# S5 tables made in their final layout from transposed powers kept in DRAM

## The chip, the cores and the metric

The kernel runs on one core of a Trainium2 chip. The metric is the device time of one execution in microseconds; three runs of the kernel before gave 1785.19 to 1787.87 us, median 1787.56.

## The reference

The program computes two layers over 512 tokens of width 2048, batch 1. Each layer is h + RMSNorm(Mixer(RMSNorm(h))). The first mixer is an S5 state-space layer, the second forgetting attention with 16 heads. The change touches the state-space part alone, with 128 groups of 16 channels and 64 states each:

```python
xn = rmsnorm(h, g_pre)
u, z = jnp.split(xn @ w_in, 2, axis=-1)
# per group: h_t = Abar h_{t-1} + Bbar u_t,  y_t = Re(C h_t) + D u_t
mag = jnp.exp(ar * dt)
abar_re, abar_im = mag * jnp.cos(ai * dt), mag * jnp.sin(ai * dt)
x_re = coef_re * bu_re - coef_im * bu_im      # Bbar u, bu = u B^T
x_im = coef_re * bu_im + coef_im * bu_re
_, _, h_re, h_im = lax.associative_scan(combine, (a_re, a_im, x_re, x_im), axis=1)
y = einsum(h_re, c_re) - einsum(h_im, c_im) + d_skip * uf
y = gelu(y); y = y * sigmoid(y @ w_glu + b_glu); y = y * silu(z)
return h + rmsnorm(y @ w_out, g_post)
```

## The kernel before

Phase A holds the projections u and z and the state-space layer. `K` is 16: there are 16 tiles of 128 channels, and 32 projections. A projection (`proj`, L174) is 48 matmuls of 128x512 in three parts, whose fp32 weights arrive in `wraw` and are split on ACT (`whi`) and DVE (`wlo`, L151) into two rounded halves. The state-space work of tile j is spread between the projections, and time is cut into 64 chunks of CL = 8 steps:

- `ssm_tables` (L402) makes BT, which takes the 8 inputs of a chunk to the state. DVE multiplies the powers of A (`apow`, partition = state) with Bbar (`B4`, made once for four tiles by `ssm_group`, L380) into `Bt` in three operations of 128x1024 (`Bt`, `btt`, `Bt`). PE transposes its 8 blocks (`btps`, L426), ACT evicts them into BT (L427). It then makes the rotations `rot` in three operations of 128x512.
- `ssm_kernel` (L443) makes `Et` (three operations of 128x1152), the 8 short convolution kernels `kps` on PE (L466), and `ktp`, which SP writes to the DRAM tile `kd` (L473) and reads back as the 8 blocks of `M` (L477).
- `ssm_u` (L479) scales u, writes it to DRAM as `ub` and reads it back as `U`.
- `ssm_scan` (L491) multiplies U by BT into `xps` (L499), and DVE does the rotation, the scan and the rotation back into `hst`.
- `ssm_y` (L518) adds M times U (L528, the M part, 16 matmuls) and Et times `hst` (L534, the H part, 32 matmuls) into `yps`.

`order_a` (L579) writes the sequence of these steps down by hand; the framework's scheduler then places every instruction in its engine's list, and its buffers come from pools (PSUM: 3 banks for projections, 5 for all else). In each list an instruction waits for its inputs and everything behind it waits too. SP's list holds the DMA issues of kd, M, ub, U and the group inputs; the weights go through POOL's. `rows` (L295) spreads the norms by four plain matmuls with the identity (L304), once in phase A. The powers and the phasors are computed by `ssm_params` (L310) on DVE in the first 50 us.

Of the kernel before, what the change touches and what calls it, by code (L numbers as in the profile page):

```python
# [11 lines left out]
F32 = mybir.dt.float32  # L12
# [10 lines left out]
NQ = 4  # L23
# [41 lines left out]
class Kern:  # L65
# [244 lines left out]
    def ssm_params(self, i):  # L310
        nc, NG = self.nc, self.NG
        sp = self.sp
        A, E, R, CO = self.AP, self.E, self.R, self.CO
        s1 = sp.tile([P, 16, NG], F32, tag="Bt", name="scr1")
        s2 = sp.tile([P, 17, NG], F32, tag="tmp", name="scr2")
        s3 = sp.tile([P, 15, NG], F32, tag="BT", name="scr3")
        ar, ai, ld, dt, x, t, n, r, q, mag, den, nr = (s1[:, k, :] for k in range(12))
        th3, cs3, sn3 = (s2[:, k:k + 3] for k in (8, 11, 14))
        nc.scalar.dma_start(s1[:, 0:3, :], i["ssm_a"])
# [58 lines left out]
        self.ts(E[:, :, 1, 0], E[:, :, 1, 2], -1.0, ALU.mult)  # L378

    def ssm_group(self, i, q0, nq):  # L380

        nc, sp = self.nc, self.sp
        bc = [P, nq, 32]
        B4 = self.B4 = sp.tile([P, nq, 3, 16], F32, tag="B4", name="B4")
        Ca = sp.tile([P, nq, 16, 2], F32, tag="Ca", name="Ca")
        Cb = sp.tile([P, nq, 16, 2], F32, tag="Cb", name="Cb")
        self.C4 = [v.rearrange("p q c s -> p q (c s)") for v in (Ca, Cb)]
        braw = sp.tile([P, nq, 3, 16], F32, tag="braw", name="braw")
        nc.sync.dma_start(braw[:, :, 1:3], i["ssm_b"][:, q0:q0 + nq])
        nc.sync.dma_start(Ca, i["ssm_c"][:, q0:q0 + nq])  # L390
        self.act(braw[:, :, 0], braw[:, :, 2], scale=-1.0)
        co = lambda c: self.CO[:, c, q0:q0 + nq].unsqueeze(2).to_broadcast(bc)
        two = lambda v, s: v[:, :, s:s + 2].rearrange("p q s c -> p q (s c)")
        t = sp.tile(bc, F32, tag="tmp", name="gt")
        self.tt(two(B4, 1), two(braw, 1), co(0), ALU.mult)
        self.tt(t, two(braw, 0), co(1), ALU.mult)
        self.tt(two(B4, 1), two(B4, 1), t, ALU.add)
        self.act(B4[:, :, 0], B4[:, :, 2], scale=-1.0)
        self.act(Cb, Ca[:, :, :, ::-1], scale=-1.0)
        self.act(Ca[:, :, :, 1], Ca[:, :, :, 1], scale=-1.0)  # L400

    def ssm_tables(self, i, j):  # L402

        nc, sp = self.nc, self.sp
        if j % 4 == 0:
            self.ssm_group(i, NQ * j, min(4 * NQ, self.NG - NQ * j))
        ql = NQ * (j % 4)
# [3 lines left out]
        Bt = sp.tile([P, NQ, 2, 16, CL], F32, tag="Bt", name="Bt")
        bv = Bt.rearrange("p q s c t -> p q (s c) t")
        bc = [P, NQ, 32, CL]
        pw = lambda c: self.AP[:, c, qs, 0:CL].unsqueeze(2).to_broadcast(bc)
        vv = lambda s: self.B4[:, ql:ql + NQ, s:s + 2].rearrange("p q s c -> p q (s c)").unsqueeze(3).to_broadcast(bc)
        t = sp.tile(bc, F32, tag="tmp", name="btt")
        self.tt(bv, pw(0), vv(1), ALU.mult)
        self.tt(t, pw(1), vv(0), ALU.mult)
        self.tt(bv, bv, t, ALU.add)

        BT = T["BT"] = sp.tile([P, NQ, 2, P], F32, tag="BT", name="BT")
        for q0 in range(0, NQ, 2):
            bps = self.bank(name="btps").rearrange("p (q c g) -> p q c g", q=2, c=2)
            for q in range(2):
                for c in range(2):
                    nc.tensor.transpose(bps[:, q, c, :], Bt[:, q0 + q, c].rearrange("p c t -> p (c t)"), self.ident)  # L426
            self.act(BT[:, q0:q0 + 2], bps)  # L427

        rot = T["rot"] = sp.tile([P, NQ, 3, NC], F32, tag="rot", name="rot")
        rv = rot[:, :, 1:3].rearrange("p q s (a b) -> p q (s a) b", b=8)  # L430
        bc = [P, NQ, 16, 8]
        e8 = lambda s: self.E[:, qs, 1, s:s + 2].rearrange("p q s a -> p q (s a)").unsqueeze(3).to_broadcast(bc)
        e1 = lambda s: self.E[:, qs, 0, 1 + s].unsqueeze(2).to_broadcast(bc)
        t = sp.tile(bc, F32, tag="tmp", name="rt")
        self.tt(rv, e8(1), e1(0), ALU.mult)
        self.tt(t, e8(0), e1(1), ALU.mult)
        self.tt(rv, rv, t, ALU.add)
        self.act(rot[:, :, 0], rot[:, :, 2], scale=-1.0)
        dec = T["dec"] = self.dec[j % 2]
        self.act(dec[:, :, :, 1:], self.R[:, qs].unsqueeze(2).unsqueeze(3).to_broadcast([P, NQ, 2, NC - 1]))  # L440
        return T

    def ssm_kernel(self, j, T):  # L443

        nc, sp = self.nc, self.sp
# [12 lines left out]
        bb = self.bb[j % 2]  # L458
        for h in range(2):
            ph = slice(64 * h, 64 * h + 64)  # L460
            self.act(bb[ph, :, :, h, :], self.B4[ph, ql:ql + NQ, 1:3])
# [29 lines left out]
    def ssm_scan(self, j, U, T):  # L491
# [3 lines left out]
        for q in range(NQ):  # L495
            for c in range(2):
                for g in range(2):
                    pg = slice(64 * g, 64 * g + 64)
                    nc.tensor.matmul(X[pg, q, c], lhsT=T["BT"][:, q, c, pg], rhs=U[:, 2 * q + g, :],  # L499
                                     start=True, stop=True)  # L500
        rot = T["rot"]
        bc = [P, NQ, 2, NC]
# [76 lines left out]
    def order_a(self):  # L579
# [5 lines left out]
        seq += [("u", j) for j in range(min(2, K))]  # L585
        z = n0
        seq += [("z", j) for j in range(max(1, n0 - 1), n0)]
        seq += [("tab", 0), ("ker", 0)]
        for s in range(K):
            seq.append(("scan", s))  # L590
            if s + 2 < K:
# [4 lines left out]
            if s + 1 == K:  # L596
                seq.append(("y", s))
                continue
            seq.append(("tab", s + 1))
            tail = [("y", s), ("ker", s + 1)]  # L600
            while z < K - n1 and (z - n0) < (K - n0 - n1) * (s + 1) / K:
                seq.append(("z", z))
# [5 lines left out]
    def phase_a(self, i):  # L608
        nc, K, D, tc = self.nc, self.K, self.D, self.tc
        self.NG = NQ * K  # L610
        with ExitStack() as ctx:
            sp = self.sp = ctx.enter_context(tc.tile_pool(name="ssm", bufs=1))
            self.AP = sp.tile([P, 2, self.NG, CL + 1], F32, name="apow")
            self.E = sp.tile([P, self.NG, 2, 3, 8], F32, name="phasors")
# [4 lines left out]
            xin = [("ga", 1), ("gt", 1), ("X", 1), ("Z", 1), ("rt2", 1), ("gy", 2), ("gy", 2),  # L619
                   ("u", 2), ("u", 2), ("U", 3), ("U", 3), ("U", 3), ("rot", 1), ("braw", 1),  # L620
                   ("zt", 2), ("zt", 2)]
            assert K <= len(xin)


            zero = sp.tile([P, S], F32, tag="BT", name="zero")
            nc.vector.memset(zero, 0.0)
            warm = self.bank(name="warm")
            for _ in range(5):
# [63 lines left out]
            for n, (c, j) in enumerate(seq):  # L692
# [466 lines left out]
```

## Time and profile before

| | us |
|---|---|
| median of three runs | 1787.56 (1785.19 to 1787.87) |
| the profiled run, its own time | 1786.9 |
| its span | 1785.1 |
| PE busy | 1762.5 (99%) |
| DVE busy | 1078.4 (60%) |
| ACT busy | 590.1 (33%) |
| POOL busy | 430.0 (24%) |

Phase A takes the first 430 us or so. PE is the engine for matrix products, DVE the vector engine, ACT the scalar engine; SP and POOL here issue DMAs. A row of a timeline gives start and length; a PE row's length runs past the start of the next one, so what an instruction takes is read from start to start. "x8" counts records: a plain fp32 matmul leaves two, a transpose one.

### The profile page before, as it was taken

To read this page: it belongs to the slowest core of one execution; us is meant where nothing else is said; L and a number is where in the kernel's file an instruction comes from. 1 tells how busy PE (TensorE), PEld (TensorE's weight loads), DVE (VectorE), ACT (ScalarE), POOL (GpSimd) and SP (SyncE) were. 2 spreads that over 40 slices of the span, in tenths; PEclk is the share of its full clock that TensorE was granted. 3 is DMA by queue.
4 is the path that set the end of the run, shared out by engine and by line. 5 is a ranking of instruction groups with operands and counts; after the bars stand their busy time and mean duration, and the time that the engine had idled before them with its cause. 6 is when DMAs were issued, how large, how long until landed. Compare 5 with 4: busy or idle time off the path is not lost.

```text
span 1785.1 us, 26466 instructions
## 1 busy us (share of the span) xinstructions
PE 1762.5 (99%) x10710; PEld 1493.7 (84%) x10710; DVE 1078.4 (60%) x1582; ACT 590.1 (33%) x993; POOL 430.0 (24%) x382
## 2 busy tenths in 40 slices
PE   9999999999999999999999999999999999999997
PEld 6888888888888888899888888888888888988887
DVE  9789898984655532365663666465655665552235
ACT  7233233323444422234332333233333332332231
POOL 1123333333100000013333343333343343300000
PEclk9999999999999999999999999999999999999999
DMA  9545555557444643342322323332223233235332
GB/s 329 151 140 158 156 161 151 146 148 242 142 144 147 209 137 96 110 148 94 94 88 89 95 89 95 95 97 92 88 89 100 89 89 96 88 129 165 102 106 95
DMA packets 126427, 226.66 MB, mean 127 GB/s; under 512 B 38496, under 2 KB 65392, under 8 KB 126048
## 3 DMA queue, kind: packets, MB, share of 16 engines
q1 hardware_dynamic: 107824, 169.59, 30.4%
q0 software_dynamic: 18192, 55.01, 10.3%
q8 instruction: 84, 1.38, 0.3%
q14 instruction: 39, 0.32, 0.1%
q10 hardware_dynamic: 288, 0.36, 0.1%
HBM read 201.88 MB, written 22.97 MB: 126 GB/s over the span
## 4 chain that ended last, share of the span: by engine, by line
PE 92%; DVE 5%; DMA 2%; issue 1%; ACT 0%; SPq 0%; POOL 0%; DVEq 0%; ACTq 0%; POOLq 0%
PE proj L170 18%; PE proj L172 18%; PE proj L171 18%; PE tok L232 6%; PE tok L231 6%; PE tok L230 6%; PE v L204 3%; PE v L205 3%; PE v L206 3%; PE yps L534 1%; PE t L943 1%; PE yps L528 1%; PE xps L499 1%; DVE wlo L151 1%; PE btps L426 1%; DVE al L75 1%
## 5 line engine op out<-in xcount | busy, mean ns | idle before, releaser
L151 DVE TENSOR_TENSOR wlo<-wraw,whi 128x1024 fp32r<-128x1024 f32 x284 | 421.1, 1484 | 461.4 <-ACT whi L84 460.2
L84 ACT ACTIVATE whi<-wraw 128x1024 fp32r<-128x1024 f32 (+2 forms) x292 | 306.0, 1049 | 873.4 <-PE proj L172 535.1
L147 POOL TENSOR_TENSOR wraw<-wraw,vecs 128x1024 f32<-128x1024 f32 (+1 forms) x128 | 263.8, 2061 | 624.5 <-DMA wraw<-kv_k 257.0
L171 PE MATMUL proj<-BH,wlo 128*128 128x512 f32 (+1 forms) x816 | 308.8, 378 | 4.3 <-DVE wlo L151 4.3
L170 PE MATMUL proj<-BH,whi 128*128 128x512 f32 (+1 forms) x816 | 310.7, 381 | 0.0
L172 PE MATMUL proj<-BL,whi 128*128 128x512 f32 (+1 forms) x816 | 308.9, 379 | 0.0
L170 PE MATMUL proj<-ah,whi 128*128 128x512 f32 x768 | 302.2, 394 | 1.3 <-ACT zt L84 1.3
L172 PE MATMUL proj<-al,whi 128*128 128x512 f32 x768 | 299.0, 390 | 0.9 <-issue 0.9
L171 PE MATMUL proj<-ah,wlo 128*128 128x512 f32 x768 | 299.2, 390 | 0.6 <-DVE wlo L151 0.6
L171 PEld LDWEIGHTS proj<-BH,wlo 128*128 128x128 f32 x816 | 154.6, 189 | 33.1 <-DVE wlo L151 5.4
L172 PEld LDWEIGHTS proj<-BL,whi 128*128 128x128 f32 x816 | 154.4, 189 | 28.8 <-DVE BL L72 0.2
L170 PEld LDWEIGHTS proj<-BH,whi 128*128 128x128 f32 x816 | 154.5, 189 | 27.5
L170 PEld LDWEIGHTS proj<-ah,whi 128*128 128x128 f32 x768 | 144.1, 188 | 33.3 <-ACT zt L84 1.7
L171 PEld LDWEIGHTS proj<-ah,wlo 128*128 128x128 f32 x768 | 144.2, 188 | 30.9 <-DVE wlo L151 1.4
L172 PEld LDWEIGHTS proj<-al,whi 128*128 128x128 f32 x768 | 144.2, 188 | 30.4
L205 PE MATMUL v<-wlo,BH 128*128 128x512 f32 (+2 forms) x320 | 111.3, 348 | 0.0
L204 PE MATMUL v<-whi,BH 128*128 128x512 f32 (+2 forms) x320 | 111.3, 348 | 0.0
L206 PE MATMUL v<-whi,BL 128*128 128x512 f32 (+2 forms) x320 | 111.3, 348 | 0.0
L230 PE MATMUL tok<-whi,BH 128*128 128x512 f32 (+1 forms) x320 | 111.1, 347 | 0.0
L230 PE MATMUL tok<-whi,ah 128*128 128x512 f32 (+1 forms) x320 | 111.0, 347 | 0.0
L232 PE MATMUL tok<-whi,al 128*128 128x512 f32 (+1 forms) x320 | 110.9, 347 | 0.0
L231 PE MATMUL tok<-wlo,ah 128*128 128x512 f32 (+1 forms) x320 | 110.9, 347 | 0.0
(213 smaller groups left out, 2395.4 us busy)
## 6 DMA issues: line engine op xcount, KB each, us to landing
wraw<-w_fox SPq DMA_DIRECT2D x64, 512.0 KB, 3.6
wraw<-w_in POOLq DMA_DIRECT2D x58, 512.0 KB, 4.3
wraw<-w_glu POOLq DMA_DIRECT2D x32, 512.0 KB, 4.5
wraw<-w_out SPq DMA_DIRECT2D x32, 512.0 KB, 3.7
wraw<-kv_k SPq DMA_DIRECT2D x32, 512.0 KB, 3.7
wraw<-w_fo SPq DMA_DIRECT2D x32, 512.0 KB, 3.6
wraw<-kv_v SPq DMA_DIRECT2D x28, 512.0 KB, 3.7
M<-kd SPq DMA_DIRECT2D x128, 64.0 KB, 2.3
```

Source lines behind the costliest of these rows:

```text
L84: self.nc.scalar.activation(out, in_, f, **kw)
L147: (eng or nc.vector).tensor_tensor(raw, raw, scale.unsqueeze(2).to_broadcast(shp), op=ALU.mult)
L151: (eng if eng and scale is None else nc.vector).tensor_tensor(lo, raw, hi, op=ALU.subtract)
L170: mm(ps, lhsT=hi, rhs=xh, start=(k == 0), stop=False)
L171: mm(ps, lhsT=lo, rhs=xh, start=False, stop=False)
L172: mm(ps, lhsT=hi, rhs=xl, start=False, stop=(k == self.K - 1))
L204: nc.tensor.matmul(o, lhsT=xh[k][:, bs], rhs=hi, start=(k == 0), stop=False)
L205: nc.tensor.matmul(o, lhsT=xh[k][:, bs], rhs=lo, start=False, stop=False)
L206: nc.tensor.matmul(o, lhsT=xl[k][:, bs], rhs=hi, start=False, stop=(k == K - 1))
L230: nc.tensor.matmul(ps, lhsT=xh[k][:, bs], rhs=hi, start=(k == 0), stop=False)
L231: nc.tensor.matmul(ps, lhsT=xh[k][:, bs], rhs=lo, start=False, stop=False)
L232: nc.tensor.matmul(ps, lhsT=xl[k][:, bs], rhs=hi, start=False, stop=(k == K - 1))
```

## The change

Powers and Bbar are turned once, instead of their product in every tile. After `ssm_params`, the new `ssm_powers` multiplies each of the 8 powers (real and imaginary) by the identity, 16 matmuls (`aps`), evicts them into `asb` on ACT and writes three tables, at_d (real, minus imaginary, imaginary), to DRAM. `ssm_group_b` makes Bbar for four tiles (`B2`), transposes it in 4 blocks (`bps`) and writes bt_d. `ssm_fetch` reads, for one tile, three blocks of at_d (`AT`) and two of bt_d (`BTab`) of 128x512 each, with rows repeated over partitions. `ssm_tables` multiplies these two straight into BT in its final layout with three operations of 128x1024, issues the fetch of the next tile, and makes `rot`. BT and rot have two buffers each, and `order_a` runs the tables two tiles ahead of the scan, one more than before. Phasors, a few buffer tags and the place of the C tables' loads change with it.

```diff
-        B4 = self.B4 = sp.tile([P, nq, 3, 16], F32, tag="B4", name="B4")
+    def ssm_powers(self):
+        nc, NG = self.nc, self.NG
+        ph, n = P // NG, CL * NG // P
+        o = self.sp.tile([P, 3, n, P], F32, tag="AT", name="asb")
+        for c in range(2):
+            ps = self.bank(name="aps").rearrange("p (n f) -> p n f", f=P)[:, :n]
+            for t in range(CL):
+                r = slice(NG * (t % ph), NG * (t % ph) + NG)
+                nc.tensor.matmul(ps[r, t // ph], lhsT=self.AP[:, c, :, t], rhs=self.ident, start=True, stop=True)
+            self.act(o[:, 2 * c], ps)
+            if c:
+                self.act(o[:, 1], ps, scale=-1.0)
+        for c in range(3):
+            nc.sync.dma_start(self.at_d[c].rearrange("(n r) q f -> (r q) n f", r=ph), o[:, c])
+
+    def ssm_group_b(self, i, n):
...
+        nc.sync.dma_start(braw, i["ssm_b"][:, q0:q0 + nq])
...
+        self.tt(t, braw[:, :, ::-1], co(self.CO[:, 2:0:-1]), ALU.mult)
+        self.tt(braw, braw, co(self.CO[:, 0:1].to_broadcast([P, 2, self.NG])), ALU.mult)
+        self.tt(B2.rearrange("p j s q -> p j q s"), jq(braw), jq(t), ALU.add)
+        ps = self.bank(name="bps").rearrange("p (j f) -> p j f", f=P)[:, :nt]
+        for j in range(nt):
+            nc.tensor.transpose(ps[:, j], B2[:, j].rearrange("p s q -> p (s q)"), self.ident)
+        o = sp.tile([P, nt, P], F32, tag="zt", name="bsb", bufs=2)
+        self.act(o, ps)
+        nc.sync.dma_start(self.bt_d[n].rearrange("j r f -> r j f"), o)
+
+    def ssm_fetch(self, j):
+        AT = sp.tile([P, 3, n], F32, tag="AT", name="AT")
+        BT = sp.tile([P, 2, n], F32, tag="BTab", name="BTab")
+        for c in range(3):
+            s = self.at_d[c]
+            nc.sync.dma_start(AT[:, c], bass.AP(s.tensor, s.offset + j * n, [[0, 16], [self.NG * P, CL], [1, n]]))
+        s = self.bt_d[j // 4][j % 4]
+        for c in range(2):
+            nc.sync.dma_start(BT[:, c], bass.AP(s.tensor, s.offset + c * 16 * n, [[n, 16], [0, CL], [1, n]]))
+        self.tabs = AT, BT
 def ssm_tables(self, i, j):
-        self.tt(bv, pw(0), vv(1), ALU.mult)
-        self.tt(t, pw(1), vv(0), ALU.mult)
-        self.tt(bv, bv, t, ALU.add)
-        BT = T["BT"] = sp.tile([P, NQ, 2, P], F32, tag="BT", name="BT")
-        for q0 in range(0, NQ, 2):
-            bps = self.bank(name="btps").rearrange("p (q c g) -> p q c g", q=2, c=2)
-            for q in range(2):
-                for c in range(2):
-                    nc.tensor.transpose(bps[:, q, c, :], Bt[:, q0 + q, c].rearrange("p c t -> p (c t)"), self.ident)
-            self.act(BT[:, q0:q0 + 2], bps)
+        AT, Bb = self.tabs
+        BT = T["BT"] = sp.tile([P, 2, n], F32, tag="BT", name="BT", bufs=2)
+        t = sp.tile([P, 2, n], F32, tag="tmp", name="btt")
+        self.tt(BT, AT[:, 0:1].to_broadcast([P, 2, n]), Bb, ALU.mult)
+        self.tt(t, AT[:, 1:3], Bb[:, ::-1], ALU.mult)
+        self.tt(BT, BT, t, ALU.add)
+        if j + 1 < K:
+            self.ssm_fetch(j + 1)
-        rot = T["rot"] = sp.tile([P, NQ, 3, NC], F32, tag="rot", name="rot")
+        rot = T["rot"] = sp.tile([P, NQ, 3, NC], F32, tag="rot", name="rot", bufs=2)
+        if j + 2 < K and (j + 2) % 4 == 0:
+            self.ssm_group_b(i, (j + 2) // 4)
 def order_a(self):
-        seq += [("tab", 0), ("ker", 0)]
+        seq += [("tab", 0), ("ker", 0)] + [("tab", 1)] * (K > 1)
-            seq.append(("tab", s + 1))
+            seq += [("tab", s + 2)] * (s + 2 < K)
```

What stands on the engines changes in more places than the diff shows. On PE, before, behind xps of tile 1 come 48 projection rows, a btps block, and then yps of tile 1 (the numbers in yps and ah name buffers; the last rows before yps):

```order
L170 MATMUL proj<-ah_269,whi 128x512
L171 MATMUL proj<-ah_269,wlo 128x512
L172 MATMUL proj<-al_270,whi 128x512
L426 MATMUL btps<-ident,Bt 128x128 x8
L528 MATMUL yps_1378<-U,M 64x64 x2
L528 MATMUL yps_1379<-U,M 64x64 x2
```

In the changed kernel, the same place, from xps of tile 1:

```order
L542 MATMUL xps<-U,BT 64x64 x16
L171 MATMUL proj<-ah_261,wlo 128x512
L172 MATMUL proj<-al_262,whi 128x512
L170 MATMUL proj<-ah_270,whi 128x512
L171 MATMUL proj<-ah_270,wlo 128x512
L571 MATMUL yps_1440<-U,M 64x64 x2
L172 MATMUL proj<-al_271,whi 128x512
L170 MATMUL proj<-ah_276,whi 128x512
L571 MATMUL yps_1441<-U,M 64x64 x2
L171 MATMUL proj<-ah_276,wlo 128x512
L172 MATMUL proj<-al_277,whi 128x512
```

The M part of yps moved from 48 projection rows behind xps to 4 rows behind it, and its pairs stand one by one between projection rows. In tile 3 it stands 5 rows behind, in tile 5 9, in tile 7 30; in tiles 9 and 11 to 15 it stands 46 or 48 rows behind, as before.

On SP, before, from the first kd write (tile 0) to the one of tile 1:

```order
L473 DMA kd<-ktp_131 128x240
L477 DMA M<-kd 128x1x128 x8
L486 DMA ub<-u 128x512
L488 DMA U<-ub 128x8x64
L473 DMA kd<-ktp_132 128x240
```

In the changed kernel, the same stretch:

```order
L516 DMA kd<-ktp_138 128x240
L443 DMA AT<-at_d_117 128x1x512
L443 DMA AT<-at_d_118 128x1x512
L520 DMA M<-kd 128x1x128 x8
L443 DMA AT<-at_d_119 128x1x512
L446 DMA BTab<-bt_d_120 128x1x512 x2
L443 DMA AT<-at_d_117 128x1x512
L443 DMA AT<-at_d_118 128x1x512
L443 DMA AT<-at_d_119 128x1x512
L446 DMA BTab<-bt_d_120 128x1x512 x2
```

The fetches of two tiles now stand between the kd write of tile 0 and that of tile 1, and the last three issues of the first of them behind the 8 issues of M.

## Rows read from the trace of the kernel before

**Rows 1.** The page's 40 slices: busy tenths of each engine

```profile
PE   9999999999999999999999999999999999999997
DVE  9789898984655532365663666465655665552235
```

**Rows 2.** One stretch: us; busy us (instructions) of PE, PEld, DVE, ACT, POOL; clock; DMA

```profile
100.00:200.00 100.00, 100.00 (x966) 83.20 (x964) 88.58 (x99) 33.70 (x60) 28.61 (x49) 1.00 0.54 153
```

**Rows 3.** Timeline of PE, tile 0: start, length, engine, line, operation

```profile
88.59 0.39 PE L171 MATMUL proj<-ah,wlo 128*128 128x512 f32 x1
...
89.05 1.03 PE L426 MATMUL btps<-ident,Bt 128*128 128x128 f32 x8
90.01 0.67 PE L466 MATMUL kps<-Et,bb 128*32 128x128 f32 x16
90.61 0.50 PE L170 MATMUL proj<-ah,whi 128*128 128x512 f32 x1
90.94 0.40 PE L171 MATMUL proj<-ah,wlo 128*128 128x512 f32 x1
...
91.51 1.15 PE L499 MATMUL xps<-U,BT 128*64 128x64 f32 x32
92.59 0.50 PE L170 MATMUL proj<-ah,whi 128*128 128x512 f32 x1
```

**Rows 4.** Timeline of PE, the norms' rows

```profile
66.34 1.06 PE L304 MATMUL rows<-ident,rs_b 128*128 128x128 f32 x8
67.16 0.47 PE L170 MATMUL proj<-ah,whi 128*128 128x512 f32 x1
```

**Rows 5.** Waits of PE, whole run: us in total, times, longest

```profile
PE proj L170 <- ACT zt L84: 1.3, 1, 1.3
PE yps L528 <- DMA M<-kd: 0.9, 1, 0.9
```

**Rows 6.** Timelines of PE and of SP's queue, and the page's DMA issues

```profile
199.76 0.39 PE L172 MATMUL proj<-al,whi 128*128 128x512 f32 x1
200.08 0.67 PE L466 MATMUL kps<-Et,bb 128*32 128x128 f32 x16
200.68 1.15 PE L528 MATMUL yps<-U,M 128*64 128x64 f32 x32
...
202.88 0.51 PE L499 MATMUL xps<-U,BT 128*64 128x64 f32 x10
...
179.12 0.32 SPq L473 DMA_DIRECT2D kd<-ktp  x1
...
201.91 0.32 SPq L473 DMA_DIRECT2D kd<-ktp  x1
205.61 5.01 SPq L477 DMA_DIRECT2D M<-kd  x8
...
221.76 0.39 SPq L473 DMA_DIRECT2D kd<-ktp  x1
...
M<-kd SPq DMA_DIRECT2D x128, 64.0 KB, 2.3
...
U<-ub SPq DMA_DIRECT2D x16, 256.0 KB, 4.4
```

**Rows 7.** Groups of DVE from 91 to 412 us: busy us, mean ns, idle before

```profile
L72 DVE TENSOR_TENSOR Bt<-apow,B 128x1024 f32<-128x1024 f32 x15 | 18.3, 1220 | 4.5 <-PE btps L426 4.2
...
L75 DVE SCALAR_TENSOR_TENSOR ktp<-eye,vecs,kps 128x16 f32<-128x16 f32 x16 | 3.6, 228 | 22.0 <-PE kps L466 22.0
```

**Rows 8.** Timeline of PE around its longest wait; 15 steps between the last two

```profile
856.91 0.28 PE L172 MATMUL proj<-BL,whi 128*128 128x256 f32 x1
857.03 0.28 PE L170 MATMUL proj<-BH,whi 128*128 128x256 f32 x1
860.90 0.58 PE L171 MATMUL proj<-BH,wlo 128*128 128x256 f32 x1 [3.60 <-DVE wlo L151]
...
864.27 0.29 PE L171 MATMUL proj<-BH,wlo 128*128 128x256 f32 x1
```

More of the change, by code (lines that the diff above doesn't have):

```diff
@@ L313, in ssm_params @@
         A, E, R, CO = self.AP, self.E, self.R, self.CO
-        s1 = sp.tile([P, 16, NG], F32, tag="Bt", name="scr1")
+        s1 = sp.tile([P, 16, NG], F32, tag="BTab", name="scr1")
         s2 = sp.tile([P, 17, NG], F32, tag="tmp", name="scr2")
-        s3 = sp.tile([P, 15, NG], F32, tag="BT", name="scr3")
+        s3 = sp.tile([P, 15, NG], F32, tag="BT", name="scr3", bufs=2)
         ar, ai, ld, dt, x, t, n, r, q, mag, den, nr = (s1[:, k, :] for k in range(12))
@@ L345, in ssm_params @@
         self.tt(CO[:, 1, :], t, den, ALU.mult)
+        self.ts(CO[:, 2, :], CO[:, 1, :], -1.0, ALU.mult)
         w1, w2 = (s2[:, x:x + 4, :].rearrange("p a g -> p (a g)").rearrange("p (g a) -> p g a", a=4) for x in (0, 4))
@@ L362, in ssm_params @@
         self.tt(R, t, t, ALU.mult)
-        c, si = E[:, :, :, 1], E[:, :, :, 2]
+        c, si = E[:, :, 0:4:3], E[:, :, 1:5:3]
         nc.vector.memset(c[:, :, :, 0], 1.0)
@@ L377, in ssm_params @@
         self.cmul(*e(slice(5, 8)), *e(slice(1, 4)), *b4, w3, w4)
-        self.ts(E[:, :, 1, 0], E[:, :, 1, 2], -1.0, ALU.mult)
-    def ssm_group(self, i, q0, nq):
-        nc, sp = self.nc, self.sp
-        bc = [P, nq, 32]
-        B4 = self.B4 = sp.tile([P, nq, 3, 16], F32, tag="B4", name="B4")
+        self.ts(E[:, :, 2], E[:, :, 4], -1.0, ALU.mult)
+        self.ssm_powers()
+    def ssm_powers(self):
[12 more added lines that the diff above has]
+            nc.sync.dma_start(self.at_d[c].rearrange("(n r) q f -> (r q) n f", r=ph), o[:, c])
@@ new lines, in ssm_group_b @@
+    def ssm_group_b(self, i, n):
+        nc, sp = self.nc, self.sp
+        nt = min(4, self.K - 4 * n)
+        nq = NQ * nt
+        q0 = 4 * NQ * n
+        braw = sp.tile([P, nq, 2, 16], F32, tag="braw", name="braw")
+        nc.sync.dma_start(braw, i["ssm_b"][:, q0:q0 + nq])
+        bc = [P, nq, 2, 16]
+        co = lambda v: v[:, :, q0:q0 + nq].rearrange("p s q -> p q s").unsqueeze(3).to_broadcast(bc)
+        t = sp.tile(bc, F32, tag="tmp", name="gt")
+        B2 = self.B2[n] = sp.tile([P, nt, 32, NQ], F32, tag="B2", name="B2", bufs=2)
+        jq = lambda v: v.rearrange("p (j q) s c -> p j q (s c)", q=NQ)
+        self.tt(t, braw[:, :, ::-1], co(self.CO[:, 2:0:-1]), ALU.mult)
[7 more added lines that the diff above has]
+        nc.sync.dma_start(self.bt_d[n].rearrange("j r f -> r j f"), o)
@@ L385, in ssm_group, with ssm_group_c @@
+    def ssm_group_c(self, i, n):
+        nc, sp = self.nc, self.sp
+        nq = NQ * min(4, self.K - 4 * n)
+        q0 = 4 * NQ * n
         Ca = sp.tile([P, nq, 16, 2], F32, tag="Ca", name="Ca")
@@ L387, in ssm_group @@
         self.C4 = [v.rearrange("p q c s -> p q (c s)") for v in (Ca, Cb)]
-        braw = sp.tile([P, nq, 3, 16], F32, tag="braw", name="braw")
-        nc.sync.dma_start(braw[:, :, 1:3], i["ssm_b"][:, q0:q0 + nq])
         nc.sync.dma_start(Ca, i["ssm_c"][:, q0:q0 + nq])
[L391 to L398, printed above, removed]
         self.act(Cb, Ca[:, :, :, ::-1], scale=-1.0)
         self.act(Ca[:, :, :, 1], Ca[:, :, :, 1], scale=-1.0)
-    def ssm_tables(self, i, j):
[L404 to L407, printed above, removed]
+    def ssm_fetch(self, j):
+        nc, sp = self.nc, self.sp
+        n = NQ * P
+        AT = sp.tile([P, 3, n], F32, tag="AT", name="AT")
[7 more added lines that the diff above has]
+        self.tabs = AT, BT
@@ L408, in ssm_tables @@
+    def ssm_tables(self, i, j):
+        nc, sp, K = self.nc, self.sp, self.K
+        if j == 0:
+            self.ssm_group_b(i, 0)
+            self.ssm_fetch(0)
+            self.ssm_group_c(i, 0)
         qs = slice(NQ * j, NQ * j + NQ)
         T = {}
[L411 to L415, printed above, removed]
@@ L429, in ssm_tables @@
-        rot = T["rot"] = sp.tile([P, NQ, 3, NC], F32, tag="rot", name="rot")
+        n = NQ * P
+        AT, Bb = self.tabs
[7 more added lines that the diff above has]
+        rot = T["rot"] = sp.tile([P, NQ, 3, NC], F32, tag="rot", name="rot", bufs=2)
@@ L430, in ssm_tables @@
         rv = rot[:, :, 1:3].rearrange("p q s (a b) -> p q (s a) b", b=8)
         bc = [P, NQ, 16, 8]
-        e8 = lambda s: self.E[:, qs, 1, s:s + 2].rearrange("p q s a -> p q (s a)").unsqueeze(3).to_broadcast(bc)
-        e1 = lambda s: self.E[:, qs, 0, 1 + s].unsqueeze(2).to_broadcast(bc)
+        e8 = lambda s: self.E[:, qs, 2 + s:4 + s].rearrange("p q s a -> p q (s a)").unsqueeze(3).to_broadcast(bc)
+        e1 = lambda s: self.E[:, qs, s].unsqueeze(2).to_broadcast(bc)
         t = sp.tile(bc, F32, tag="tmp", name="rt")
@@ L458, in ssm_kernel @@
         bb = self.bb[j % 2]
+        B2 = self.B2[j // 4][:, j % 4].rearrange("p (s c) q -> p q s c", s=2)
         for h in range(2):
             ph = slice(64 * h, 64 * h + 64)
-            self.act(bb[ph, :, :, h, :], self.B4[ph, ql:ql + NQ, 1:3])
+            self.act(bb[ph, :, :, h, :], B2[ph])
         kps = self.bank(name="kps")[:, :P]
@@ L498, in ssm_scan @@
                     pg = slice(64 * g, 64 * g + 64)
-                    nc.tensor.matmul(X[pg, q, c], lhsT=T["BT"][:, q, c, pg], rhs=U[:, 2 * q + g, :],
+                    nc.tensor.matmul(X[pg, q, c], lhsT=T["BT"][:, c, q * P + 64 * g:q * P + 64 * g + 64], rhs=U[:, 2 * q + g, :],
                                      start=True, stop=True)
@@ L613, in phase_a @@
             self.AP = sp.tile([P, 2, self.NG, CL + 1], F32, name="apow")
-            self.E = sp.tile([P, self.NG, 2, 3, 8], F32, name="phasors")
+            self.E = sp.tile([P, self.NG, 5, 8], F32, name="phasors")
+            self.at_d = [self.dp.tile([CL, self.NG, P], F32, name=f"at_d{c}") for c in range(3)]
+            self.bt_d = [self.dp.tile([min(4, K - 4 * n), P, P], F32, name=f"bt_d{n}") for n in range((K + 3) // 4)]
+            self.B2 = {}
             self.R = sp.tile([P, self.NG], F32, name="rdec")
@@ L618, in phase_a @@
             ws = [((c, j), i["w_in"][j + (K if c == "z" else 0)], None) for c, j in seq if c in "uz"]
-            xin = [("ga", 1), ("gt", 1), ("X", 1), ("Z", 1), ("rt2", 1), ("gy", 2), ("gy", 2),
-                   ("u", 2), ("u", 2), ("U", 3), ("U", 3), ("U", 3), ("rot", 1), ("braw", 1),
+            xin = [("X", 1), ("Z", 1), ("rt2", 1), ("gy", 2), ("gy", 2), ("u", 2), ("u", 2),
+                   ("U", 3), ("U", 3), ("U", 3), ("rot", 2), ("rot", 2), ("braw", 1), ("Ca", 1),
                    ("zt", 2), ("zt", 2)]
             assert K <= len(xin)
-            zero = sp.tile([P, S], F32, tag="BT", name="zero")
+            zero = sp.tile([P, S], F32, tag="BT", name="zero", bufs=2)
             nc.vector.memset(zero, 0.0)
@@ L707, in phase_a @@
                     if j == 0:
-                        self.rows(rstd, self.rstd, sp, "gt", True)
+                        self.rows(rstd, self.rstd, sp, "rt2", True)
                     U[j] = self.ssm_u(j, ps)
@@ L713, in phase_a @@
                     self.ssm_kernel(j, T[j])
+                    if j + 1 < K and (j + 1) % 4 == 0:
+                        self.ssm_group_c(i, (j + 1) // 4)
                 elif c == "scan":
```

1 line of the change is left out of this document (removed).

## Prediction

> **What bounds the kernel now.** I read first the page's slices: PE is at 9 tenths from the second slice to the last, DVE at 8 or 9 only in the first quarter [rows 1]. So the program ends when PE has worked through its list, and an instruction that leaves PE's list gives its time back unless PE then waits. Next, a table of stretches: from 100 to 200 us, where the SSM tiles run between projections, PE is busy in all 100 us and DVE in 88.6, at full granted clock and a DMA share of 0.54 [rows 2]. PE binds there, with DVE 11% behind it; every microsecond of PE's list in this stretch reaches the end. PE's waits come third: in the whole run one of 1.3 us on zt, which stands at 43 us, and one of 0.9 us on M [rows 5]. There is thus little waiting to win back, and a new wait costs its full length. The sum is made against the profiled run, 1786.9 us, 0.7 below the median of 1787.56; I make no correction for that. I call 0.2%, 3.6 us, the least difference that a measurement of this kernel can tell from none.
>
> **Work removed from PE.** 16 blocks btps of 8 transposes go. In the timeline one takes from 89.05 to 90.01, 0.96 us [rows 3]. Without it the next SSM row pays the step from a projection row that btps pays now, 0.31 (199.76 to kps at 200.08) instead of the 0.23 between projection rows (two steps from 88.59 to 89.05), 0.08 [rows 3, 6]. That leaves 0.88 each: **-14.1 us**. The 32 ACT evictions behind them go too; ACT is not what PE waits for, so they are worth nothing. The zt wait goes because aps rows and a different weight order now fill that place: **-1.3**.
>
> **Work added to PE.** ssm_powers multiplies the powers by the identity in 16 plain matmuls. The nearest rows are the four of the rows block: 66.34 to 67.16, 0.82 us, 0.205 each [rows 4], so 3.3. They stand alone at 11 places more than one, between projections; a return from a foreign block costs its first projection row 0.33 instead of 0.23 (90.61 to 90.94) [rows 3], so some 0.12 for each place, 1.4. Together **+4.7** (3.3 to 5.6). Four blocks bps of 4 transposes, half a btps block, 0.47 each: **+1.9**. The powers on DVE must be ready for aps about half a microsecond before they are now: **+0.5** (0 to 2).
>
> The trace shows that plain multiplications by the identity come out as two records each (8 for 4 matmuls, [rows 4]) and transposes as one (8 for 8, [rows 3]). The Trainium skill, "Perfetto Trace Analysis", section Transposes, asks for transposes in place of ordinary matmuls; the trace agrees. With transposes at 0.96 / 8 = 0.12 the 16 would cost 1.9 instead of 3.3; the sum keeps 3.3, since the change uses the plain form.
>
> **Work split on PE.** The order shows more than the removal: the M part of yps for tiles 1, 3 and 5 stands in 8 pairs with one or two projection rows between each, where before its 16 matmuls were one block. Rows price such a split: three projection rows between kps and xps take 90.61 to 91.51, 0.90 us, against 3 x 0.23 = 0.69 [rows 3], so 0.21 for a pair of switches. With 7 extra pairs in each of three tiles and two or three in tile 7, some 24 x 0.19: **+4.5** (2.5 to 5).
>
> **A wait that M brings.** This carries the forecast. M(j) is read back from kd, which is written from ktp, which comes from kps(j). Before, 48 projection rows stood between xps(j) and yps(j). Now kps(1), yps(0) and xps(1) stand together and only 4 projection rows follow before the first pair of yps(1); 5 in tile 3, 9 in tile 5, 30 in tile 7. PE reaches that pair after kps 0.60, yps(0) 2.20 (200.68 to 202.88), xps 1.08 and 4 rows, 1.0: 4.9 us from the start of kps [rows 3, 6]. The data: from kps at 200.08 to the issue of kd at 201.91 is 1.8, from there to the first M issue at 205.61 is 3.7, and M lands 2.3 after its issue [rows 6]. That is 7.8 us, so PE waits 2.9 in tile 1. In tile 3 it reaches the pair at 5.1 and waits 2.7, in tile 5 at 6.0 and 1.8. The 8 M issues take 5.0 us, the last starting 4.4 after the first, so it lands at 12.2; in tile 7 PE wants it at about 11.7 and waits 0.5 to 1. Sum **+8.2**. Below: kd's issue could come 1 us sooner where nothing stands ahead of ktp on DVE and ACT (kps takes only 0.60 of the 1.8), which leaves 4. Above: the extra traffic lengthens landings. The change fetches five transfers of 256 KB per tile, 1.31 MB in about 20 us, 65 GB/s on the 153 shown [rows 2]; U, of the same size, lands in 4.4 us [rows 6]. One microsecond more in each of two hops over four tiles makes 14 to 16.
>
> By the Trainium skill, "DMA: Bandwidth & Descriptors", section Anatomy of one DMA, a transfer costs about 2 us plus its bytes over 436 GB/s; an estimate from it puts kd at 2.3 and U at 2.6, where rows have 3.7 up to the next issue for kd and 4.4 for U. By the page the M waits would be about 1.4 us shorter in each of the first three tiles and gone in tile 7, some 5 in all; the rows decide.
>
> **Waits on the fetch.** SP issues in order. The last three issues of the fetch for tile 2 stand behind the 8 M issues of tile 0 (and so in later tiles). M(0) ends its issues about 1.8 + 3.7 + 5.0 = 10.5 us after kps(0); three issues of 0.5 or so and 4.4 to land make 16.5 [rows 6]. Behind it on DVE stand three table operations, three rotations and three for B2 (the first like Bt, 1.22 each [rows 7], the others half as wide, 0.6 each), 7.3 us, and between them the wlo operations, which are as wide as Bt: 24 to 26 with one or two of those. PE reaches bps of the second group 93 rows and xps later, at about 23. I take **+3** (0 to 5), and for kps of tiles 0, 2 and 4, whose Et stands behind the same DVE queue, **+2** (0 to 4). That DVE queue also holds ktp, and behind ktp the kd write, M and yps: a late fetch is passed on.
>
> **DVE close behind.** A pair of tiles takes 42.6 us (179.12 to 221.76) with 144 projection rows [rows 6]. In the new order the pairs from tile 2 to 9 hold about 121. PE's need falls to 121 x 0.23 + 2 x 4.2 = 36.2; DVE's is 0.886 x 42.6 = 37.8 less one wlo, 36.6. In these pairs PE could not run at its own pace even if M were there. The waits and splits above bring PE to some 39, so I add nothing, but it keeps the saving from being whole: DVE spends 22.0 us waiting for kps already [rows 7].
>
> **Sum.** -14.1 - 1.3 + 4.7 + 1.9 + 0.5 + 4.5 + 8.2 + 3 + 2 = +9.4, so 1796.
>
> **The rivals.**
> (a) *The data are there in time.* If M and the fetches land before PE asks, what remains is -14.1 - 1.3 + 4.7 + 1.9 + 0.5 + 4.5 = -3.8: 1783, faster. For it: M waits were 0.9 in the whole run before [rows 5], and DMA has room (share 0.54). Against: the 48 rows that hid M are gone in three tiles. It decides where M's first issue follows kd's within 0.8 us in tile 1, 1.0 in tile 3 and 1.9 in tile 5, instead of 3.7. Chance 0.16.
> (b) *The waits are half as long* (4 + 1 + 1) and the splits cost 2.5: -3.8 - 2 + 6, about no change, 1787. Chance 0.19.
> (c) *Waits drop the clock.* After a wait of 3.60 us, rows of 256 columns take 3.37 us for 15 steps, 0.225 each, where 0.12 stood between them before it [rows 8]; that is the lower level of the granted clock, 1.2 GHz, and costs 1.6. After 1.3 us at 43 us nothing like it is seen. Waits of 2.9 and 2.7 stand between. If four waits reach that length, with longer landings and M waits near 14, +9.4 + 5.8 + 6 less what overlaps, 1: 1807. Chance 0.20. The Trainium skill, "TensorE: Matmul & The Clock Gate", section Why this matters for your kernels, says that idle gaps between bursts bring the low clock back; the trace agrees.
> (d) *The change does not do what it says*, the btps time staying in another form, is excluded by the order: no btps rows stand there.
> The forecast itself, 1790 to 1801, has 0.45.
>
> **How the numbers follow.** Predicted is the forecast's 1796. Range: the low end reaches into (a), 1782, the high end to most of (c), 1806; a tenth is left out on either side. The forecast's own range is 1790 to 1801. Faster is (a), 0.16; same is (b), 0.19; slower the forecast and (c), 0.65.
>
> **What would show it.** In the new profile: no btps; aps and bps near 5 and 2 us busy; PE waits on M in yps of tiles 1, 3, 5 of 2 to 3 us each, a wait at the second bps, and DVE waits for AT or BTab. Granted clock below 1.00 in 100 to 300 us would be (c). If M waits are under 0.5 us each, the forecast's main step is wrong; if PE waits on DVE more than on M, the co-bound is what I mis-sized.

## The result, and the profile after

The change makes the kernel slower: median 1844.46 us of four runs (1840.94 to 1847.55) against 1787.71 before, a ratio of 1.0319 with a 95% interval of 1.0307 to 1.0332. The sign was forecast, the size was not: the predicted loss was 8 us and the range ended at 1806; the measured loss is 57.

The profiled run of the changed kernel took 1847.55 us, the longest of the four. Its page, with the rows that answer to [rows 1] and the granted clock under them:

```profile
PE   9998988899999999999999999999999999999997
...
DVE  8567778888365542238655566645663666552235
...
PEclk9998889999999999999999999999999999999999
```

Four of PE's slices from the fourth to the eighth have become 8s, and the granted clock stands at 8 in the fourth to sixth. That is phase A. All of the loss lies there: between the profiled runs the last yps starts its last row at 483.5 us instead of 421.6, and the first v matmul of phase D at 879.5 instead of 818.0, 61.5 later; the whole span is 60.7 longer.

The waits of PE from 75 to 500 us (total, times, longest), where before there were 0.9 on M [rows 5] and 0.9 on issue:

```profile
PE yps L571 <- DMA M<-kd: 14.5, 9, 4.3
PE kps L509 <- DVE Et L72: 8.0, 6, 3.5
PE bps L417 <- DVE B L72: 5.6, 3, 4.6
PE proj L170 <- ACT gy L84: 1.4, 1, 1.4
```

And what DVE waited for in that stretch, the table transfers, which is new:

```profile
DVE btt L72 <- DMA BTab<-bt_d: 25.5, 8, 5.0
...
DVE BT L72 <- DMA BTab<-bt_d: 8.1, 3, 3.9
```

Three stretches of 25 us with the columns of [rows 2] (us, busy us by engine, granted clock, DMA share, GB/s) show the rest:

```profile
150.00:175.00 25.00, 23.44 (x255) 16.04 (x250) 13.77 (x17) 6.44 (x11) 6.26 (x11) 0.73 0.55 151
200.00:225.00 25.00, 21.65 (x148) 14.28 (x145) 15.09 (x20) 4.63 (x9) 6.61 (x12) 0.73 0.52 144
250.00:275.00 25.00, 20.75 (x154) 13.27 (x149) 13.46 (x17) 3.09 (x7) 6.84 (x13) 0.66 0.57 156
```

PE is idle for 1.6 to 4.2 us in each, and the mean granted clock is 0.73 or less. At its lower level, 1.2 GHz, the record is 0.5, so 0.73 over 25 us is 13.5 us at that level. Summed over the 25 us stretches from 75 to 500 us, PE is idle for 31.7 us (1.8 before) and TensorE stands at 1.2 GHz for 65 us (0 before). A microsecond at half speed loses half a microsecond, so idle and clock together cost 30 + 32 = 62 us, or some 60, since 4 us of the idle lie inside stretches at 1.2 GHz and are counted twice. That is the whole loss between the profiled runs, 60.7. The work on PE is thus about as long as before. That what btps saved went into aps, bps and the split follows from the sum; no run times the split at full clock.

What this looks like on PE behind xps of tile 1, the place shown in the orders ahead of the prediction:

```profile
153.24 0.40 PE L170 MATMUL proj<-ah,whi 128*128 128x512 f32 x1
153.48 0.40 PE L171 MATMUL proj<-ah,wlo 128*128 128x512 f32 x1
155.43 0.34 PE L571 MATMUL yps<-U,M 128*64 128x64 f32 x4 [1.56 <-DMA M<-kd]
155.69 0.50 PE L172 MATMUL proj<-al,whi 128*128 128x512 f32 x1
156.03 0.40 PE L170 MATMUL proj<-ah,whi 128*128 128x512 f32 x1
156.36 0.43 PE L571 MATMUL yps<-U,M 128*64 128x64 f32 x4
156.72 0.80 PE L171 MATMUL proj<-ah,wlo 128*128 128x512 f32 x1
157.31 0.63 PE L172 MATMUL proj<-al,whi 128*128 128x512 f32 x1
157.87 0.48 PE L571 MATMUL yps<-U,M 128*64 128x64 f32 x4
158.29 0.80 PE L170 MATMUL proj<-ah,whi 128*128 128x512 f32 x1
159.01 0.48 PE L571 MATMUL yps<-U,M 128*64 128x64 f32 x4
```

The wait on M is there, 1.56 us where 2.9 was predicted (from the issue of kd at 150.73 to the first M issue at 152.52 it took 1.8 us here, not 3.7). What follows was not predicted: from 156.4 on a group of one projection row and one pair takes 1.14 us (157.87 to 159.01) and one of two rows and a pair 1.5, where the first group of two rows and a pair, still at full speed, took 0.93 (155.43 to 156.36). PE is not waiting here; it runs at half speed, and goes on so until about 170 us, some 5 us beyond the end of the M part.

### The profile page after: what moved, and what is told of

It is laid out like the page before. It is cut to its first block, busy times and chain, and to the rows that moved or that the text cites. A ratio compares the mean times of both kernels' runs of the same rounds, so it can differ in the third digit from the quotient of the medians.

```text
span 1845.8 us, 26390 instructions
## 1 busy us (share of the span) xinstructions
PE 1795.8 (97%) x10630; PEld 1500.8 (81%) x10630; DVE 1082.0 (59%) x1583; ACT 580.2 (31%) x960; POOL 420.7 (23%) x382
## 3 DMA queue, kind: packets, MB, share of 16 engines
q1 hardware_dynamic: 115360, 192.41, 33.6%
## 4 chain that ended last, share of the span: by engine, by line
PE 83%; DVE 6%; DMA 5%; SPq 2%; issue 2%; ACT 1%; DVEq 0%; ACTq 0%
PE proj L171 16%; PE proj L170 16%; PE proj L172 16%; PE tok L230 6%; PE tok L231 6%; PE tok L232 6%; PE v L205 3%; PE v L204 3%; PE v L206 3%; DMA BTab<-bt_d 3%; DVE wlo L151 1%; SPq L520 1%; DMA M<-kd 1%; PE t L992 1%; DMA kd<-ktp 1%
## 5 line engine op out<-in xcount | busy, mean ns | idle before, releaser
L147 POOL TENSOR_TENSOR wraw<-wraw,vecs 128x1024 f32<-128x1024 f32 (+1 forms) x128 | 259.7, 2029 | 635.0 <-DMA wraw<-kv_k 274.6
L170 PE MATMUL proj<-ah,whi 128*128 128x512 f32 x768 | 309.4, 403 | 1.8 <-ACT gy L84 1.4
L171 PE MATMUL proj<-ah,wlo 128*128 128x512 f32 x768 | 309.2, 403 | 0.7 <-DVE wlo L151 0.7
L172 PE MATMUL proj<-al,whi 128*128 128x512 f32 x768 | 307.5, 401 | 0.0
L171 PEld LDWEIGHTS proj<-ah,wlo 128*128 128x128 f32 x768 | 148.4, 193 | 33.9 <-DVE wlo L151 1.9
L172 PEld LDWEIGHTS proj<-al,whi 128*128 128x128 f32 x768 | 148.0, 193 | 31.1
```

The lines of the kernel that those rows point to most:

```text
L147: (eng or nc.vector).tensor_tensor(raw, raw, scale.unsqueeze(2).to_broadcast(shp), op=ALU.mult)
L170: mm(ps, lhsT=hi, rhs=xh, start=(k == 0), stop=False)
L171: mm(ps, lhsT=lo, rhs=xh, start=False, stop=False)
L172: mm(ps, lhsT=hi, rhs=xl, start=False, stop=(k == self.K - 1))
```

## The experiments

Idle and time at 1.2 GHz are sums over the stretches from 75 to 500 us of the profiled run, as above. Times are medians, against 1785 to 1788 for the kernel before, timed beside them; e1, e2, e6, e8, e9 and e10 have two runs each, e4 three, e3 and e7 four, e5 eight.

| kernel | us | profiled run | PE idle | at 1.2 GHz |
|---|---|---|---|---|
| before | 1787 | 1787 | 1.8 | 0 |
| the change | 1844 | 1848 | 31.7 | 65.0 |
| M part in one block (e1) | 1838 | 1838 | 43.4 | 45.0 |
| no fetch (e2) | 1806 | 1803 | 16.2 | 13.5 |
| tables one tile ahead (e3) | 1826 | 1831 | 35.5 | 38.5 |
| before without btps (e4) | 1778 | 1777 | 6.0 | 0 |
| e3 without fetch (e5) | 1793 | 1788 | 10.5 | 7.0 |
| fetch on ACT's queue (e6) | 1852 | 1855 | 42.7 | 61.5 |
| e3 with two buffers, fetch two ahead (e7) | 1803 | 1801 | 12.7 | 10.5 |
| e7 on ACT's queue (e8) | 1823 | 1820 | 26.9 | 31.0 |
| filler ahead of the M part (e9) | 1829 | 1828 | 29.4 | 20.5 |
| e5 with unread traffic (e10) | 1804 | 1806 | 21.6 | 21.0 |

### e1: the M part in one block

```diff
-        for q in range(NQ):
-            for h in range(2):
+        for q in reversed(range(NQ)):
+            for h in (1, 0):
...
-                                     start=(q == 0), stop=False)
+                                     start=(q == NQ - 1), stop=False)
```

> The changed kernel with the M part of yps walked from its last block to its first, so that its first matmul needs the last of the eight M transfers and its 16 matmuls stand in one block again (20, 20, 25 and 30 projection rows behind xps in tiles 1, 3, 5 and 7). Fetches and tables are untouched. Theory A (late data): PE idles because the fetch of AT and BTab comes late to DVE and M late to PE; the idle of about 32 us between 100 and 475 us stays, and so does most of the low clock: 1830 to 1845. Theory B (the split): the pairs of yps between projection rows are what keeps TensorE's clock at its lower level for 13 us at a time; without them the granted clock is near 1.00 but for a few us behind each wait, and 20 to 30 us come back: 1812 to 1825.

1838.13 us: theory A's range. Time at 1.2 GHz fell by 20 us, which is worth 10, but PE's waits on M rose by 11:

```profile
PE yps L571 <- DMA M<-kd: 25.5, 6, 6.5
```

The three stretches from above, with the M part whole:

```profile
150.00:175.00 25.00, 18.54 (x260) 15.33 (x257) 15.25 (x18) 6.42 (x11) 7.80 (x14) 0.86 0.59 152
200.00:225.00 25.00, 18.18 (x189) 14.39 (x188) 17.20 (x20) 5.37 (x9) 10.07 (x18) 0.80 0.62 169
250.00:275.00 25.00, 21.54 (x213) 17.33 (x212) 21.83 (x26) 6.32 (x11) 8.30 (x15) 0.93 0.72 199
```

In the first of them PE waits 6.46 us for M in one piece and is at 1.2 GHz for 7 us (0.86); the split M part behind a wait of 1.56 us was at 1.2 GHz for 13.5. So the split hides M's lateness and pays for it in clock; taking it away gives the lateness back as idle. It is not the root.

### e2 and e5: no fetch, with tables two tiles or one tile ahead

```diff
-        if j + 1 < K:
-            self.ssm_fetch(j + 1)
```

> The changed kernel with the fetch of AT and BTab for tile 0 alone; tiles 1 to 15 use tile 0's tables again, so 75 transfers of 256 KB are left out and with them part of what is computed. The order still splits the M part in tiles 1 and 3 and two pairs of tile 5. Theory A (late data): DVE waits for no table, bps and kps are in time, PE's idle falls from 32 to under 12 us: 1795 to 1805. Theory B (the split): the two split tiles still run at the lower clock, 6 to 8 us each, and M waits stay: 1805 to 1820. Rival C (the fetch's traffic alone lengthens all landings, M's too): also M waits vanish, 1785.

1806.12 us (1802.66 and 1809.58), at the edge between A and B: 38 us of the 57 go with the fetch. The order stayed split in tiles 1 and 3, M waits were 8.6 us, and 13.5 us at 1.2 GHz remain.

> Tables one tile ahead as before the change, and the fetch of AT and BTab left out but for tile 0 (its tables are used for all tiles, so what is computed differs): PE's order is close to that of the kernel before and DVE waits for no transfer. It gives what the new layout alone is worth. Theory A (the fetch is what costs): at or a little below the kernel before: measured -9 for btps, +4.7 and +1.9 for aps and bps, 1782 to 1790. If the change has another cost that is neither the fetch nor the order: above 1795.

1792.92 us (eight runs, 1787.8 to 1795.6; ratio 1.0042, 1.0031 to 1.0052), above A's range by 3. With a fetch for tile 0 alone and nearly the old order, the new layout does not beat the kernel before. The trace is of the fastest run, 1787.8; in it the last yps row still comes 5.7 us later than before (427.3 instead of 421.6), and the part behind phase A, which the change does not touch, was shorter in that execution. What PE waits for is little:

```profile
PE yps L569 <- DMA M<-kd: 3.7, 4, 1.9
PE kps L507 <- DVE Et L72: 3.1, 3, 2.1
PE bps L417 <- DVE B L72: 1.5, 1, 1.5
```

### e3: tables one tile ahead

```diff
-        seq += [("tab", 0), ("ker", 0)] + [("tab", 1)] * (K > 1)
+        seq += [("tab", 0), ("ker", 0)]
...
-            seq += [("tab", s + 2)] * (s + 2 < K)
+            seq.append(("tab", s + 1))
```

> The changed kernel with the tables one tile ahead, as before the change, instead of two: layout, powers through DRAM and the fetch stay. PE's order is then nearly that of the kernel before: yps 46 to 48 projection rows behind xps, no split. Theory A: the fetch still stands behind M in SP's list and takes 6.8 us to land, DVE still waits about 30 us for it, bps, kps or xps come late: 1800 to 1815. Theory B: without the split the clock stays at 1.00 and M is in time; what remains is -14 for btps, +7 for aps and bps, and a few us of waits: 1780 to 1788.

1825.73 us, ratio 1.0211 (1.0187 to 1.0234): slower than either theory's range, but on A's side. PE's order was near that of the kernel before, no M part was split, and still PE idled 35.5 us, since the table operations on DVE stood waiting (17.3 us on BTab, 14.6 more that the trace files under issue) and Et behind them:

```profile
PE kps L509 <- DVE Et L72: 11.5, 4, 5.9
PE yps L571 <- DMA M<-kd: 9.1, 6, 4.4
```

With and without the fetch the times are 1826 and 1793 one tile ahead, at 1844 and 1806 two tiles ahead. The fetch costs 33 or 38 us, the tile further ahead 19 or 13.

### e4: what btps was worth

```diff
-        for q0 in range(0, NQ, 2):
-            bps = self.bank(name="btps").rearrange("p (q c g) -> p q c g", q=2, c=2)
...
-            self.act(BT[:, q0:q0 + 2], bps)
+        T["BT"] = Bt.rearrange("p q s c t -> p q s (c t)")
```

> The kernel before with its 128 transposes btps and the 32 evictions behind them left out (xps reads the table Bt untransposed, so its numbers are others). It measures the gain alone that the change is after. By the prediction's first term -14.1 us: 1773. Rival: DVE, busy 89% of that stretch, becomes the bound and less than half comes back: above 1780.

1778.37 us, ratio 0.9954 (0.9935 to 0.9973): -9 us, between the two expectations and two thirds of the -14.1 in the sum. PE's idle rose from 1.8 to 6.0 us, for the most part in front of kps, and that is nearly all of the missing third:

```profile
PE kps L460 <- ACT gy L84: 3.5, 7, 0.5
PE yps L522 <- DMA M<-kd: 2.3, 1, 2.3
```

The btps block had covered these waits: yps, kps and the eviction of gy come closer together once it is gone.

### e6 and e8: the fetch on ACT's queue

```diff
-            nc.sync.dma_start(AT[:, c], bass.AP(...
+            nc.scalar.dma_start(AT[:, c], bass.AP(...
```

The same is done for BTab.

> The changed kernel with the fetch's DMAs issued from ACT's queue instead of SP's, so that they no longer stand behind the eight M issues; buffers and tables two tiles ahead stay. If the place in SP's list is what makes the fetch late: DVE's waits for BTab fall from 33.6 us to under 10 and the time to 1805 to 1820. If it is the landing time (6.8 us) and the single buffer, which lets the fetch start only when DVE has read the tables before: waits stay, 1835 to 1850.

1852.18 us, no better than the change itself (8 us slower). DVE's waits for BTab fell from 33.6 to 11.6 us, as the first branch expected, and the time did not: ACT now stood in its place, its whi held behind the fetch issues (35.2 us filed under M<-kd), and wlo and PE behind whi. The place in SP's list counted, but not for the end.

> The same as the run with two buffers, the fetch issued from ACT's queue. If SP's list still delays M or the fetch there, this is 5 us or more faster than that run; if only the buffer counts, within 3 us of it. ACT loses 64 issues of about 0.6 us, which PE does not wait for.

1822.88 us, 20 slower than the same kernel with the fetch on SP. Neither branch named this: ACT is not spare in this phase, since every projection's weights pass through it. Its whi operations stood waiting behind the fetch issues (33.9 us, filed under M and AT), and DVE's waits for whi rose from 47.9 us in e7 to 67.1.

### e7: two buffers, the fetch two tiles ahead

```diff
-        AT = sp.tile([P, 3, n], F32, tag="AT", name="AT")
-        BT = sp.tile([P, 2, n], F32, tag="BTab", name="BTab")
+        AT = sp.tile([P, 2, n], F32, tag="AT", name="AT", bufs=2)
+        BT = sp.tile([P, 2, n], F32, tag="BTab", name="BTab", bufs=2)
...
-        if j + 1 < K:
-            self.ssm_fetch(j + 1)
+        if j + 2 < K:
+            self.ssm_fetch(j + 2)
```

BT and rot have one buffer again to make room, the group's Bbar is made ahead of the fetch, and four blocks a tile are fetched instead of five.

> Tables one tile ahead, the fetch two tiles ahead into two buffers of AT and BTab each, and four transfers a tile instead of five (the negative imaginary powers are not fetched; DVE subtracts instead, which splits one operation in two halves). The fetch stays on SP. If the single buffer is what made the fetch late, DVE's waits for BTab are under 3 us, PE's idle under 8 us and the clock is at 1.00: 1782 to 1792. If the traffic itself costs (M, ub and wraw landing later), PE's waits on M and wlo remain: 1800 to 1815.

1802.91 us, ratio 1.0103 (1.0086 to 1.0119): the time of the second branch, with the waits for BTab of the first. They fell to 2.4 us and PE's idle to 12.7: 23 of the 33 us that separate e3 from e5 came back with the second buffer, the earlier fetch and the fifth transfer saved, which this run does not part. The last 10 did not, although the data were in time. The order has a share in them: the M part of tile 3 stands 19 projection rows behind xps here, 41 in e5, and its last two pairs stand alone; the clock falls to 0.86 in 175 to 200 us. The landing times of this run, in the page's DMA issues, tell of the traffic:

```profile
AT<-at_d SPq DMA_DIRECT2D x32, 256.0 KB, 6.0
BTab<-bt_d SPq DMA_DIRECT2D x32, 256.0 KB, 6.4
...
ub<-u SPq DMA_DIRECT2D x16, 256.0 KB, 4.9
```

ub took 2.2 us before the change and 2.3 without the fetch (e5); BTab's 6.4 stands against 4.4 for U in [rows 6], a transfer of the same size.

### e9: work in place of the wait

```diff
...
+        if j in (1, 3, 5):
+            for x in range(24):
+                nc.tensor.matmul(yb[0][:, NQ * NC:], lhsT=self.fill[:, :P], rhs=self.fill[:, :NQ * NC], start=True, stop=True)
...
```

> The changed kernel with 24 extra matmuls of 128x256 (2.9 us at the full clock, their result overwritten by nothing that is read) ahead of the M part of yps in tiles 1, 3 and 5: PE works where it waited for M. It adds 8.6 us of work; the M part then stands nearly in one block there. If the wait ahead of the M part and the split are what takes TensorE to the lower clock for 13 us at a time, time at the lower clock falls from 65 us to 30 or less, which gives back 17, and the waits they fill give 5 more: 1828 to 1838. If the lower clock has another cause in that stretch, the extra work comes on top: 1848 to 1856.

1828.96 us, the first branch and 15 us faster than the change, with 9.2 us of PE's work more. The same three stretches as above:

```profile
150.00:175.00 25.00, 23.44 (x359) 18.83 (x358) 20.30 (x25) 8.08 (x15) 10.67 (x18) 1.00 0.65 175
200.00:225.00 25.00, 21.64 (x192) 17.11 (x193) 17.41 (x21) 5.44 (x10) 5.38 (x10) 0.80 0.56 151
250.00:275.00 25.00, 23.42 (x232) 18.76 (x230) 22.14 (x27) 6.29 (x13) 5.93 (x10) 1.00 0.71 187
```

In the first of them PE's busy time is to the hundredth that of the change (23.44), but the clock is 1.00 instead of 0.73, and the 24 filler matmuls and 47 projection rows fit in where 43 rows did. The idle is the same 1.56 us, but in five pieces of at most 0.46 instead of one. Time at 1.2 GHz fell from 65 to 20.5 us. Not all of that is the filler's: the order moved with it. The M part stands right behind xps and the filler in tile 1, 4 rows behind in tile 3, but 33 in tile 5 instead of 9 and 48 in tile 7 instead of 30. The stretch of tile 1 is the one that tells of the filler; in tile 3 a wait of 3.36 us came within the M part in spite of it, and the clock fell to 0.80. The wait and the split went together, so this run does not part the two; with e1, where the split alone went and 45 us remained, it shows that both feed the low clock.

### e10: traffic that nobody waits for

```diff
+        d = self.dp.tile([5, P, S], F32, tag="dum", name="dum", bufs=2)
+        for c in range(5 if j else 0):
+            nc.sync.dma_start(d[c], ub.rearrange("g c t k -> (g c) (t k)"))
```

> The run with tables one tile ahead and no fetch (1793), with five transfers of 256 KB a tile put back on SP's list behind U, from ub to a DRAM tile that nobody reads: traffic and issues of the fetch's size, but nothing waits for the data. PE's order is the same but for the last tile. If the fetch costs because DVE and then PE wait for its data, this stays within 5 us of 1793; if traffic or SP's longer list cost by themselves (M, U, wraw later), it comes near the 1826 of the run with the fetch: 1805 to 1830.

1804.14 us (1802.29 and 1805.99), 11 more than e5 and one below the second branch. So transfers and issues of the fetch's size cost something by themselves. The trace shows how: what stands behind them on SP's list comes later. DVE waited 6.5 us for the C table `Ca`, issued behind five of the transfers, and PE then 3.94 us for `hst` in tile 3. In tile 14 ktp was ready at 404.9, but kd was issued at 409.1, behind U and the five transfers, and PE waited 6.7 us for M although 48 projection rows stood between; only behind these waits does PE's order differ from e5's. How the 11 us divide between the longer list and the traffic on the DMA engines, this run does not show. e7, with four transfers a tile, has 10, but in another order.

## Why the prediction was wrong

**Removed work: -14.1.** Right as a count of PE time, too high as a gain: -9 alone (e4). The cover that I did not name was btps itself, standing in front of waits on gy and M.

**Added work: +4.7, +1.9, +0.5, zt -1.3.** In sum +3.9 up to the norms' rows; they start at 71.88 instead of 66.34, +5.5. A lone aps with its two turns costs about 0.6 rather than 0.33: 16 matmuls are 6.3 us busy, bps 3.0 instead of 1.9 (2.4 in e5, where the clock stayed up). A mis-sizing of 3 us.

**The split: +4.5.** Priced at full clock (and at 0.19 for each pair, where the rows gave 0.21, which is half a microsecond). At 1.2 GHz each group of a pair and a projection row cost 1.14 instead of some 0.7 (0.93 less a row of 0.23); that loss belongs to the clock, below.

**M waits: +8.2.** They were there and measured 14.5 us, at nine places and not four (1.6, 3.4 and 4.3 in tiles 1, 3 and 5, for 2.9, 2.7 and 1.8); the upper bound of 14 to 16 was the nearer. **Fetch waits: +3 and +2.** Measured 5.6 and 8.0. The mechanism (SP's list, DVE's queue, then bps, kps and M) held; DVE waited 33.6 us for BTab, whose landing I took as U's 4.4 and which was 6.8:

```profile
AT<-at_d SPq DMA_DIRECT2D x48, 256.0 KB, 5.6
BTab<-bt_d SPq DMA_DIRECT2D x32, 256.0 KB, 6.8
```

Its second reason is the single buffer: the fetch of a tile can start only when DVE has read the one before, and DVE needs it soon after. e7, with a second buffer, an earlier fetch and one transfer less, was 23 us faster than e3. The prediction spoke of the list and of traffic and not of the buffer. The Trainium skill, "DMA: Bandwidth & Descriptors", section Anatomy of one DMA, has about 2 us plus bytes over 436 GB/s for transfers issued from GpSimd, an estimate of 2.6 us for 256 KB; the tables come through SP's queue, and their measured 5.6 and 6.8 lie far above it and decide. All of PE's waits from 75 to 500 us together rose by 30 us, where the sum had 13.

**The clock.** This is the step that failed. The sum had nothing for it; rival (c) had 1.6 us for each of four waits and came to 1807, with chance 0.20. Measured were 65 us at the lower level, a loss of some 30. Of the 51 us between the sum's +9.4 and the 60.7 of the profiled runs, the clock is thus some 30, the longer waits 17, aps and bps 3. I took [rows 8], where the low clock lasted for 15 steps of unbroken projection rows, as the price of any wait. Behind the wait of tile 1 the low clock lasted for 13 us, in the first 9 of which PE went between pairs of yps and projection rows. In e1, with the M part whole, it lasted 7 us although the wait was longer; in e9, which gave PE work there and made the M part nearly whole, the stretch stayed at full clock. [rows 8] are right for the stretch that they show; that a mixed stretch behind a wait pays for longer no row of the kernel before could show. The prediction also counted two waits of PE in the whole run; [rows 5] leave out the one behind which [rows 8] stand:

```profile
PE proj L171 <- DVE wlo L151: 4.9, 4, 3.6
```

**DVE close behind.** I added nothing for it. It passed the late tables on to Et (kps, 8.0 us) and was itself no bound: it was busy 74 of the 100 us from 175 to 275.

**The rivals.** (a), data in time, would not have made the change a gain either: without fetch and with nearly the old order it stood at 1793 (e5). The rest of its sum is -3.8, and -8.3 without the split, which e5 does not have; in e5's profiled run phase A ends 5.7 us later than before. Between the two lie 9 us of new idle, some 3 for the clock and 2 for aps and bps. (c) named the right cause with a fifth of its size.

What remains open is how the 13 to 19 us of the tile further ahead divide between M's split, its waits and the order on DVE; no run isolates it. Open too is how the 33 us of the fetch one tile ahead divide between the buffer, SP's list and the traffic. No version here beats the kernel before but e4, which leaves the transposition out.

## What to carry to other kernels

Where one engine has no slack, work taken off it is worth only what stands behind it without covering another wait, and a DRAM round trip put in its place must be in time by more than one buffer's turn. Price a wait on PE with the clock behind it: look at what PE does after the wait, and if that is small matmuls between large ones, as here, count the stretch at half speed and not the wait alone: it was 13 us behind a wait of 1.56.

## What the runs showed of the hardware

A kernel with 9.2 us of matmuls more was 15 us faster: in 150 to 175 us, with the same 23.44 us of PE busy, the granted clock was 1.00 instead of 0.73 (e9; elsewhere the order had moved too). Behind a wait of 1.56 us TensorE stayed at 1.2 GHz for 13.5 us, over pairs of 64 columns between rows of 512 and then rows alone; with a wait of 6.46 us and the pairs in one block it was 7 us (e1).

Transfers of 256 KB that repeat rows over the partitions landed in 5.6 and 6.8 us, and others landed later beside them: ub went from 2.2 to 5.4 us in the changed kernel and was at 2.3 without the fetch (e5). Unread transfers of like volume, with their place on SP's list, cost 11 us (e10).
